# Sample search by sixteen candidates, two alternating row searches and whole queries in DRAM, in a two-layer hybrid decoder step

## The chip, the cores and the metric

The kernel runs on one core of one Trainium2 chip. The metric is device time in microseconds of one execution; the time of a kernel is the median of its runs. One further execution was taken by the hardware profiler, and all rows below are from that one.

## The reference

Layer 0 is a Mamba-2 branch beside a convolution branch. The change touches only layer 1, a sparse attention for 1024 prompt rows and, with the same weights, for 8 samples (one new row each, over 1024 cached keys and its own).

```
q, k, v, qi, ki, wi, z = odd_project(x, w_in)          # 1024-wide x times w_in
s = einsum('bthd,bsd->bths', qi, ki) * IDX_DIM ** -0.5   # 8 index heads of 64
scores = einsum('bths,bth->bts', relu(s), wi * IDX_HEADS ** -0.5)
scores = where(key_pos <= q_pos, scores, -inf)
_, idx = top_k(scores, 256)                             # per row
logits = einsum('btgrd,btkgd->btgrk', q, k_sel) * ATTN_HEAD_DIM ** -0.5
o = softmax(logits) @ v_sel                             # 16 heads, 4 groups of keys
y = layer_norm(ALPHA * x + (o * silu(z)) @ w_out)
```

## The kernel before

The program is written as Python loops; a scheduler puts the instructions of each engine into one fixed order before the run, and each engine then works through its own list in that order and waits where an operand is not there yet. A late operand therefore holds up everything behind it on the same engine.

Layer 1 (function `layer1`) starts near 905 us. Its first part, the front, ends near 1284 us and does three things side by side.

*Projections on TensorE (PE).* 66 pieces here called chunks, each 344 columns of one 128-row output tile: index queries QI (4 tiles of 3 chunks), queries QQ (8 tiles), keys KK (2 tiles), gates ZZ (8 tiles). fp32 accuracy is had by splitting weights and inputs in a high and a low half; a chunk is 24 matmuls (`mm3`, L132 to L134). The weights of a tile come in two parts; for each, a DMA fills `wst` (L105), ScalarE (ACT) casts the high half `whi` (L108), and VectorE (DVE), or GpSimd (POOL) where `eng=` says so, subtracts to get the low half `wlo` (L109). L132 and L133 need `whi`, L134 needs `wlo`. Queries are split in the same way as they leave PE: ACT casts the high half (L1113), DVE subtracts (L1114), and both halves go to `dq` in DRAM. Keys are split by L1132 (ACT) and L1133 (DVE), gates leave by L1186 (ACT).

*Scores.* For each block of 128 prompt rows (blocks 7 to 2; `SCORE_ROWS`), 8 index heads and up to two stretches of keys: two matmuls (L1033, L1034; 80 such pairs), relu on ACT (L1036), weighting and summing on DVE (L1040 and its neighbours) into `S`. The samples' scores come behind all blocks (matmuls L1068 to L1089) into `Ss`, 8 rows of 1025.

*Top-k by bisection on the bits of the 256th largest score.* Blocks 7, 6, 5 are searched on DVE (`topk_halves`, L1264 and what follows). Blocks 4, 3, 2 (search "a") and the samples (search "s") are searched on ACT and POOL by `topk_signs`: per bit, ACT takes the sign of score minus candidate and sums it over the row (L1231: three instructions `jka` of 640, 512 and 384 columns for "a", one `jks` of 1025 for "s"), and POOL turns the sums into the next candidate (L1236, L1250, L1251, L1253). 32 bits each. Then `masks` on DVE turns thresholds into 0/1 masks (L1306 counts, L1330 to L1334 scan and combine), in the order d, a, s.

The attention behind it goes through the blocks from 7 down. For each block and each of 4 key groups, `load_q` fetches the two halves of the queries from `dq` (L1139, into one of two `Q` buffers), PE makes logits (L1403), DVE applies the mask and takes the extremum (L1404), ACT the exponential (L1408), PE transposes and multiplies by V. POOL has the gates' products (L1465, L1467) and weight halves of the output projection (L1487). `sample_softmax` spreads the samples' masked scores over the heads by matmuls (L1578, L1584).

## Time and profile before

| | |
|---|---|
| median of 3 runs | 1689.2 us (1688.87 to 1689.37) |
| profiled execution | 1682.48 us, of which the span from first to last instruction is 1680.7 us |
| busy share of the span | PE 95%, DVE 70%, ACT 52%, POOL 20% |
| mean granted TensorE clock | 0.982 of full |
| DMA | 186.27 MB, mean 111 GB/s |
| layer 1 | front 905 to 1284 us, attention 1285 to 1681 us |

The busy shares are means over stages of different limits; what counts for the change is the front's second half, from the last score to the first logits.

### The profile page before, as it was taken

Reading aid. Unit: us, or ns where it says so; the run is one execution under the profiler, and the core shown is the slowest. Engines: PE = TensorE matmul, PEld = TensorE weight load, DVE = VectorE, ACT = ScalarE, POOL = GpSimd, SP = SyncE. Lnnn points to the kernel's source line nnn. Section 1 sums busy time; section 2 is a strip of 40 time slices with the busy share of each in tenths; the row PEclk is TensorE's granted clock in tenths of the full one; section 3 lists DMA queues with packets and bytes.
Section 4 is the critical chain, followed back from the end, with each engine's and each line's share of the span. In section 5 each row is a group of like instructions: output and inputs, shape, how many; then the busy total and the mean of one; then the engine's idle time right before and its main releaser. Section 6 shows DMA issues by size and latency. Waiting matters only on the chain. (4 is left out here: it accounts for less than half of the span.)

```text
span 1680.7 us, 28833 instructions
## 1 busy us (share of the span) xinstructions
PE 1589.8 (95%) x10334; PEld 1430.6 (85%) x10334; DVE 1170.7 (70%) x2460; ACT 869.4 (52%) x1958; POOL 335.0 (20%) x677
## 2 busy tenths in 40 slices
PE   8999989989999998999899999888898899999997
PEld 7999989989999997998899999777897576666675
DVE  4788977551466878766575568999967866565574
ACT  5255423562445555444534455577775755456563
POOL 4000000001212225123422200144361411112120
PEclk9999989999999999999999999999999999999999
DMA  7332242354112146433531214422346424543351
GB/s 236 109 118 62 69 114 92 127 175 170 40 38 63 61 141 210 129 116 101 167 106 51 92 47 135 130 95 89 120 147 186 129 48 111 136 110 89 85 131 59
DMA packets 167235, 186.27 MB, mean 111 GB/s; under 512 B 20500, under 2 KB 131436, under 8 KB 166836
## 3 DMA queue, kind: packets, MB, share of 16 engines
q1 hardware_dynamic: 164436, 178.41, 36.0%
q0 software_dynamic: 1216, 4.37, 0.8%
q8 instruction: 81, 1.33, 0.3%
q10 hardware_dynamic: 1440, 1.65, 0.3%
q14 instruction: 62, 0.51, 0.1%
HBM read 132.43 MB, written 54.05 MB: 111 GB/s over the span
## 5 line engine op out<-in xcount | busy, mean ns | idle before, releaser
L132 PE MATMUL pp<-act,whi 128*128 128x344 f32 x1016 | 328.9, 325 | 12.6 <-ACT act L233 8.2
L134 PE MATMUL pp<-act,wlo 128*128 128x344 f32 x1016 | 330.2, 327 | 10.6 <-DVE wlo L109 10.6
L133 PE MATMUL pp<-act,whi 128*128 128x344 f32 x1016 | 329.4, 324 | 0.8 <-POOL act L726 0.6
L132 PEld LDWEIGHTS pp<-act,whi 128*128 128x128 f32 x1016 | 193.2, 191 | 15.7 <-ACT act L233 8.2
L134 PEld LDWEIGHTS pp<-act,wlo 128*128 128x128 f32 x1016 | 193.6, 191 | 13.2 <-DVE wlo L109 11.5
L133 PEld LDWEIGHTS pp<-act,whi 128*128 128x128 f32 x1016 | 193.1, 190 | 3.4 <-POOL act L726 0.9
L108 ACT CAST whi<-wst 128x512 fp32r<-128x512 f32 x150 | 92.1, 617 | 151.9 <-PE pp L133 69.1
L334 DVE SCALAR_TENSOR_TENSOR uv<-uv,cst,uv 128x1024 f32<-128x1024 f32 x120 | 157.8, 1315 | 2.6
L132 PE MATMUL pp<-yh,whi 128*128 128x344 f32 x412 | 135.4, 329 | 8.4 <-DVE ev L1114 3.9
L109 DVE TENSOR_TENSOR wlo<-wst,whi 128x512 fp32r<-128x512 f32 x104 | 71.3, 691 | 98.8 <-ACT whi L108 98.7
L134 PE MATMUL pp<-yh,wlo 128*128 128x344 f32 x412 | 134.4, 326 | 3.6 <-DVE wlo L109 3.4
L1404 DVE CUSTOM_DVE_ANT_0 P<-lg,w 128x512 f32<-128x512 f32 (+3 forms) x144 | 82.8, 597 | 52.7 <-PE lg L1403 49.0
L1403 PE MATMUL lg<-w,Q 128*128 128x512 f32 (+3 forms) x384 | 104.9, 379 | 9.2 <-DVE nmx L1404 9.0
L109 POOL TENSOR_TENSOR wlo<-wst,whi 128x512 fp32r<-128x512 f32 x46 | 60.9, 1326 | 155.8 <-ACT whi L108 144.7
L132 PEld LDWEIGHTS pp<-yh,whi 128*128 128x128 f32 x412 | 79.1, 192 | 13.1 <-DVE ev L1114 5.3
L1408 ACT ACTIVATE P<-P,mx 128x1024 f32<-128x1024 f32 (+3 forms) x64 | 63.3, 989 | 49.6 <-DVE mx L1407 46.4
L1403 PEld LDWEIGHTS lg<-w,Q 128*128 128x128 f32 x384 | 64.7, 196 | 28.2 <-DVE nmx L1404 15.6
L1430 PEld LDWEIGHTS tr<-cst,P 128*128 128x128 f32 x576 | 65.7, 143 | 26.5 <-issue 20.1
L1430 PE MATMUL tr<-cst,P 128*128 128x128 f32 x576 | 86.1, 283 | 1.3 <-DVE yo L1463 1.3
L1439 PE MATMUL pv<-ph,V 128*64 128x256 f32 (+1 forms) x640 | 82.8, 375 | 2.9 <-ACT ph L1435 1.4
L134 PEld LDWEIGHTS pp<-yh,wlo 128*128 128x128 f32 x412 | 79.0, 192 | 5.2 <-DVE wlo L109 4.4
L1231 ACT ACTIVATE jka<-S,canda 128x640 bf16<-128x640 f32 (+2 forms) x96 | 68.7, 716 | 20.4 <-POOL canda L1253 15.8
(583 smaller groups left out, 3986.0 us busy)
## 6 DMA issues: line engine op xcount, KB each, us to landing
wst<-in_W SPq DMA_DIRECT2D x166, 256.0 KB, 2.8
Q<-dq SPq DMA_DIRECT2D x64, 256.0 KB, 4.2
dq<-ev SPq DMA_DIRECT2D x48, 172.0 KB, 1.8
q<-in_ck SPq DMA_DIRECT2D x64, 128.0 KB, 2.3
vp<-in_cv SPq DMA_DIRECT2D x64, 128.0 KB, 2.4
xst<-in_xT SPq DMA_DIRECT2D x8, 516.0 KB, 10.2
dzb<-ob SPq DMA_DIRECT2D x24, 172.0 KB, 1.9
uv<-dzb SPq DMA_DIRECT2D x8, 516.0 KB, 4.5
```

Source lines behind the costliest of these rows:

```text
L108: nc.scalar.copy(hi, st)
L109: (eng or nc.vector).tensor_tensor(lo, st, hi.bitcast(F32), op=ALU.subtract)
L132: nc.tensor.matmul(out, wh, ah, start=(start and kt == kts[0]), stop=False)
L133: nc.tensor.matmul(out, wh, al, start=False, stop=False)
L134: last = nc.tensor.matmul(out, wl, ah, start=False, stop=(stop and kt == kts[-1]))
L334: nc.vector.scalar_tensor_tensor(out, x, w[:, j : j + 1], y, op0=ALU.mult, op1=ALU.add)
L1231: nc.scalar.activation(jk, s, AF.Sign, bias=cand.bitcast(F32)[:, j : j + 1], scale=-1.0, accum_out=cnt[:, j : j + 1])
L1403: mm = nc.tensor.matmul(lg, Q[:, 4 * a + r, :], KT[g][:, s0 : s0 + m], start=(a == 0), stop=(a == 1))
L1404: nc.vector.tensor_tensor_reduce(out=P[:, s0 : s0 + m], in0=lg, in1=M[tb][:, s0 : s0 + m], scale=-0.125, scalar=BIG, op0=ALU.add, op1=ALU. ...
L1408: nc.scalar.activation(P, P, AF.Exp, bias=mx[:, r : r + 1], scale=-1.0, accum_out=rsum[:, r : r + 1])
L1430: nc.tensor.transpose(p[:, a, r * 128 : r * 128 + 128], Ps[r][:, (sb + a) * 128 : (sb + a) * 128 + 128], k.ident)
L1439: nc.tensor.matmul(pv[64 * u : 64 * u + 64, 256 * pr + c0 : 256 * pr + c1], V[:, sb + a, g * 64 : g * 64 + 64], ph[:, a, c0:c1], start=(sb ...
```

## The change

1. The samples' scores are now spread over 128 partitions (16 copies of each sample's row) and made right behind the first row block. Their search takes 4 bits a round: each of the 16 copies tests another candidate. A round is one Sign on ACT (128x1025), a comparison on POOL, a small matmul that counts the fitting candidates (`same`, L1165), an ACT copy, and three POOL instructions. 8 rounds in place of 32; round i is placed behind query tile i. Some 30 small instructions at the start of layer 1 make its constants.
2. The search of blocks 4, 3, 2 becomes two, "a" (block 4) and "b" (blocks 3 and 2), whose bits are issued in turn, held back until the last relu; a cast per bit goes.
3. Queries go to DRAM whole, in one fp32 copy (24 DMAs of 172 KB, not 48). `load_q` fetches half the bytes into `qst` and splits there: an ACT cast (L1220) and a POOL subtraction (L1221), 128x512 each, for all 32 loads.
4. The low weight halves of QQ, KK and ZZ (36), those of the keys (12) and the small copies L1151 go from DVE to POOL.
5. `sample_softmax` reads `Ss` directly, without its three fp32 matmuls (six instructions in the trace). A reduction of DVE (QX) moves behind the searches.

```
-    dq = k.t(dram, [4, 8, 64, T], F32, "dq")
+    dq = k.t(dram, [4, 4, 64, T], F32, "dq")
...
+    p = pm(k)[:, :128]
+    nc.tensor.matmul(p, c1("r128")[:8], c1("r128")[:8], start=True, stop=True)
+    nc.scalar.activation(same, p, AF.Copy, scale=t8[:, 3:4])
...
+        if tb == SCORE_ROWS[0]:
+            sample_scores()
...
+    def topk_samples():
...
+        for n in range(8):
+            cnt, fit, d = one("cnt"), one("fit"), one("dig")
+            nc.scalar.activation(jk[:, :1025], Ss[:, :1025], AF.Sign, bias=cand.bitcast(F32), scale=-1.0, accum_out=cnt)
+            eng.tensor_scalar(fit, cnt, float(1025 - 2 * TOPK), None, op0=ALU.is_le)
+            p = pm(k)[:, :1]
+            nc.tensor.matmul(p, same, fit, start=True, stop=True)
+            nc.scalar.copy(d, p)
...
+                eng.tensor_scalar(by, d, step[:, n : n + 1], None, op0=ALU.mult)
+                eng.tensor_tensor(new, base, by, op=ALU.add)
...
+                eng.tensor_tensor(cand, base, ups[:, n + 1 : n + 2], op=ALU.add)
+            yield base
...
     for i in range(8):
-        w = load_w(k, A["W"][QQ + i])
+        w = load_w(k, A["W"][QQ + i], eng=nc.gpsimd)
         for t0, n in CH:
-            p = pp(k)
+            p = pp(k) if i < 3 else either()
             mm3(k, p, w, x1, t0, n)
-            hi, lo = ev(F32R), ev(F32R)
-            nc.scalar.copy(hi, p)
-            nc.vector.tensor_tensor(lo, p, hi.bitcast(F32), op=ALU.subtract)
...
+            q = ev()
+            nc.scalar.copy(q, p)
...
+        ts = next(ss)
...
-        w = load_w(k, A["W"][KK + i])
+        w = load_w(k, A["W"][KK + i], eng=nc.gpsimd)
...
+            for j in range(2):
+                kt, here, there = KT[2 * i + j], slice(64 * j, 64 * j + 64), slice(64 - 64 * j, 128 - 64 * j)
+                nc.gpsimd.tensor_tensor(kt[there, sl], kf[here], kt[here, sl].bitcast(F32), op=ALU.subtract)
+
     def load_q(tb, g):
+
+        st = k.t(QB, [128, 512], F32, "qst", 1).rearrange("p (h t) -> p h t", h=4)
+        for j in range(2):
+            nc.sync.dma_start(st[64 * j : 64 * j + 64], dq[g][:, :, tb * 128 : tb * 128 + 128].rearrange("h d t -> d h t"))
         q = qb()[:, :1024].rearrange("p (h t) -> p h t", h=8)
-        for j in range(2):
-            nc.sync.dma_start(q[64 * j : 64 * j + 64].bitcast(F32),
-                              dq[g][:, :, tb * 128 : tb * 128 + 128].rearrange("h d t -> d h t"))
+        nc.scalar.copy(q[:, 0:4], st)
+        nc.gpsimd.tensor_tensor(q[:, 4:8], st, q[:, 0:4].bitcast(F32), op=ALU.subtract)
         return q
...
-        w = load_w(k, A["W"][ZZ + i])
+        w = load_w(k, A["W"][ZZ + i], eng=nc.gpsimd)
...
-    a, d = blocks(ACT_ROWS), blocks(DVE_ROWS)
-    ta = topk_signs("a", 128, a)
+    a, b, d = blocks(ACT_ROWS[:1]), blocks(ACT_ROWS[1:]), blocks(DVE_ROWS)
+    sa, sb = topk_signs("a", 128, a), topk_signs("b", 128, b)
+    for n in range(32):
+        with tc.issue_after(relu.ins) if n == 0 else ExitStack():
+            ta, tb = next(sa), next(sb)
...
-            nc.tensor.matmul(lg, R8, Ss[:, hf * 512 : hf * 512 + 512], start=True, stop=True)
             x = SL[:, hf * 512 : hf * 512 + 512]
-            nc.vector.tensor_tensor(x, x, lg, op=ALU.add)
+            nc.vector.tensor_tensor(x, x, Ss[:, hf * 512 : hf * 512 + 512], op=ALU.add)
```

**Order on ACT, at the second and first chunks of the gate tile ZZ0.** Before, the Signs of "a" (`jka`) and "s" (`jks`) alternate between the gate evictions (L1186):

```order
L1186 ACTIVATE ev_11710<-pp_11685 128x344
L1231 ACTIVATE jks_14046,cnts_14045<-Ss_9952,cands_14038 8x1025
L1231 ACTIVATE jka_13007,cnta_13004<-S_9951,canda_12995 128x512
L108 CAST whi_11923<-wst_11921 128x512
L1186 ACTIVATE ev_11738<-pt_11713 128x344
L1231 ACTIVATE jks_14056,cnts_14055<-Ss_9952,cands_14048 8x1025
L1231 ACTIVATE jka_13009,cnta_13004<-S_9951,canda_12995 128x384
```

In the changed kernel, at the same tile, gate evictions are L1256, and the Sign of block 4 (`canda`) alternates with the two of blocks 3 and 2 (`candb`):

```order
L1256 ACTIVATE ev_11772<-pp_11747 128x344
L1302 ACTIVATE jka_13328,cnta_13327<-S_10005,canda_13309 128x640
L1256 ACTIVATE ev_11800<-pt_11775 128x344
L1302 ACTIVATE jka_13337,cntb_13336<-S_10005,candb_13320 128x512
L108 CAST whi_11881<-wst_11879 128x512
L1302 ACTIVATE jka_13339,cntb_13336<-S_10005,candb_13320 128x384
L108 CAST whi_12013<-wst_12011 128x512
L1256 ACTIVATE ev_11828<-pp_11803 128x344
```

The samples' Signs have gone from here; the last Sign of "a" and "b" now stands beside ZZ3's second chunk, with 13 gate chunks of PE behind it, where before it stood beside ZZ6.

**Order on POOL, beside the last query tiles.** Before, POOL had only the steps of the two searches there:

```order
L1236 TENSOR_SCALAR bya_12965<-cnta_12956,fstepa_12757 128x1
L1236 TENSOR_SCALAR bys_13960<-cnts_13955,fsteps_13738 8x1
L1253 TENSOR_TENSOR cands_13958<-lows_13959,bys_13960 8x1
L1251 TENSOR_TENSOR lows_13969<-cands_13958,lows_13969 8x1
L1250 CAST lows_13979<-fsteps_13738 8x1
```

Now weight halves (`wlo`) and the samples' steps (`bys`, `bases`, `cands`) stand between the steps of "a" and "b":

```order
L109 TENSOR_TENSOR wlo_11268<-wst_11265,whi_11267 128x512
L1307 TENSOR_SCALAR byb_13070<-cntb_13063,fstepb_12896 128x1
L1174 TENSOR_SCALAR bys_11143<-digs_11136,steps_10678 128x1
L1175 TENSOR_TENSOR bases_11142<-bases_11031,bys_11143 128x1
L109 TENSOR_TENSOR wlo_11373<-wst_11370,whi_11372 128x512
L1324 TENSOR_TENSOR candb_13068<-lowb_13069,byb_13070 128x2
L1179 TENSOR_TENSOR cands_11146<-bases_11142,upss_10679 128x1
L1232 COPY q_11713<-qs_9165 64x2x4 x2
L1307 TENSOR_SCALAR bya_13080<-cnta_13075,fstepa_12847 128x1
```

A search step that stands behind a `wlo` waits for it, and a `wlo` waits for the steps ahead of it.

**Order on PE, at the last scores.** Before, projection matmuls (L132 to L134) stand between the last score pairs (L1033, L1034):

```order
L133 MATMUL pp_10974<-yb_8238,whi_10964 128x344
L1033 MATMUL pt_10435<-ki_9191,Q_9860 128x384
L1034 MATMUL pt_10435<-ki_9192,Q_9860 128x384
L134 MATMUL pp_10974<-yh_8237,wlo_10965 128x344
L132 MATMUL pp_10974<-yh_8239,whi_10964 128x344
```

Now the last eight pairs (L1118, L1119) follow each other, and the first of the counting matmuls (L1165) comes behind them:

```order
L1118 MATMUL pt_10562<-ki_9233,Q_9901 128x384
L1119 MATMUL pt_10562<-ki_9234,Q_9901 128x384
L1118 MATMUL pt_10568<-ki_9233,Q_9902 128x384
L1119 MATMUL pt_10568<-ki_9234,Q_9902 128x384
L1143 MATMUL pt_10574<-ev_10576 128x512
L1165 MATMUL pm_10686<-fits_10682,same_9228 128x1
```

Counted over the whole order, 24.1 chunks stood ahead of the last score pair and 41.9 behind it; now 22.5 stand ahead and 43.5 behind.

## Rows read from the trace of the kernel before

**Rows 1.** Busy time of each engine (with its instructions) in stretches of layer 1, then the granted PE clock, the share of DMA time and GB/s. The four columns behind the window's length and PE are PEld, DVE, ACT and POOL. The second stretch is from the last scores to the end of the projections, the third the hand-over to attention.

```profile
1000.00:1060.00 60.00, 60.00 (x356) 56.97 (x355) 55.02 (x112) 35.55 (x77) 1.05 (x3) 1.00 0.39 117
1060.00:1284.00 224.00, 199.57 (x1363) 186.55 (x1361) 190.67 (x428) 153.51 (x361) 89.25 (x326) 0.96 0.39 117
1284.00:1310.00 26.00, 19.01 (x116) 12.59 (x116) 25.29 (x57) 13.81 (x19) 1.05 (x1) 0.80 0.79 226
1310.00:1660.00 350.00, 344.36 (x2298) 244.34 (x2295) 221.07 (x687) 203.60 (x451) 67.15 (x82) 1.00 0.42 102
```

**Rows 2.** PE's timeline: start, duration, line, and in brackets the idle time ahead and what ended it. Last score pair, two matmuls of the last chunk, first and fifth logits.

```profile
1070.38 0.38 PE L1034 MATMUL pt<-ki,Q 128*128 128x384 f32 x1
...
1282.73 0.32 PE L133 MATMUL pp<-yl,whi 128*128 128x344 f32 x1
...
1283.84 0.32 PE L134 MATMUL pp<-yh,wlo 128*128 128x344 f32 x1
...
1285.10 1.20 PE L1403 MATMUL lg<-w,Q 128*128 128x512 f32 x4
1290.96 0.80 PE L1403 MATMUL lg<-w,Q 128*128 128x512 f32 x1 [4.66 <-DVE nmx L1404]
```

**Rows 3.** What PE waits for between 1060 and 1285 us: total us, times, longest.

```profile
PE pt L134 <- DVE wlo L109: 6.4, 4, 3.8
PE pp L132 <- DVE ev L1114: 3.9, 5, 1.3
PE pp L134 <- DVE wlo L109: 3.4, 2, 2.6
PE pt L132 <- DVE w L1133: 2.6, 1, 2.6
```

**Rows 4.** PE's groups between 1070.4 and 1284.5 us: the samples' part of the work (L1166 is the samples' logits, L1068 and L1086 their scores).

```profile
L1166 PE MATMUL pt<-q,q 128*32 128x128 f32 x240 | 9.6, 276 | 0.0
L1068 PE MATMUL pt<-w,q 128*64 128x128 f32 x64 | 8.1, 292 | 0.0
L1086 PE MATMUL pt<-q,W 64*8 64x512 f32 x4 | 1.9, 590 | 0.0
```

**Rows 5.** ACT's groups between 1060 and 1285 us: busy us, mean ns of one, idle time ahead and what ended it.

```profile
L1231 ACT ACTIVATE jka<-S,canda 128x512 bf16<-128x512 f32 (+2 forms) x95 | 67.9, 715 | 20.4 <-POOL canda L1253 15.8 <-DVE S L1040 2.0 <-POOL canda L1248 1.8
L1231 ACT ACTIVATE jks<-Ss,cands 8x1025 bf16<-8x1025 f32 x32 | 36.7, 1148 | 2.8 <-DVE Ss L1091 1.8 <-POOL cands L1253 0.9
```

**Rows 6.** ACT's timeline late in search "a": a Sign that waited for POOL, the read of its sum, an eviction, a Sign, a weight cast, a Sign; each next one starts while the end of the one before is still shown.

```profile
1258.94 0.83 ACT L1231 ACTIVATE jka<-S,canda 128x640 bf16<-128x640 f32 x1 [0.69 <-POOL canda L1253]
1259.67 0.18 ACT L1231 ACTIVATION_READ_ACCUMULATOR jka<-S,canda 128x1 f32 x1
1259.76 0.44 ACT L1186 ACTIVATE ev<-pt 128x344 f32<-128x344 f32 x1
1260.10 0.71 ACT L1231 ACTIVATE jka<-S,canda 128x512 bf16<-128x512 f32 x1
1260.71 0.19 ACT L1231 ACTIVATION_READ_ACCUMULATOR jka<-S,canda 128x1 f32 x1
1260.81 0.60 ACT L108 CAST whi<-wst 128x512 fp32r<-128x512 f32 x1
1261.32 0.61 ACT L1231 ACTIVATE jka<-S,canda 128x384 bf16<-128x384 f32 x1
```

**Rows 7.** POOL: the step L1236 of search "a" between 1060 and 1243 us (DVE busy nearly throughout) and between 1245 and 1285 us (DVE mostly idle), and the weight halves that POOL makes in layer 0.

```profile
L1236 POOL TENSOR_SCALAR bya<-cnta,fstepa 128x1 int32<-128x1 f32 x67 | 30.2, 452 | 27.4 <-ACT jka L1231 26.5
...
L1236 POOL TENSOR_SCALAR bya<-cnta,fstepa 128x1 int32<-128x1 f32 x24 | 6.9, 290 | 14.8 <-ACT jka L1231 14.8
...
L109 POOL TENSOR_TENSOR wlo<-wst,whi 128x512 fp32r<-128x512 f32 x46 | 60.9, 1326 | 155.8 <-ACT whi L108 144.7
```

**Rows 8.** DVE's groups between 1060 and 1285 us that leave it with the change.

```profile
L109 DVE TENSOR_TENSOR wlo<-wst,whi 128x512 fp32r<-128x512 f32 x27 | 18.5, 687 | 17.1 <-ACT whi L108 17.1
L1114 DVE TENSOR_TENSOR ev<-pp,ev 128x344 fp32r<-128x344 f32 x14 | 7.2, 511 | 0.0
```

**Rows 9.** DVE's timeline: the last score sum, the end of masks "d", the first and last instruction of masks "a", the first count of masks "s".

```profile
1079.03 0.62 DVE L1040 SCALAR_TENSOR_TENSOR S<-cum,wi,S 128x384 f32<-128x384 f32 x1
...
1242.41 0.96 DVE L1334 TENSOR_TENSOR w<-cum,eq 128x768 bf16<-128x768 f32 x1
...
1272.92 0.88 DVE L1306 TENSOR_SCALAR_CACHE_REDUCE eq<-S,canda 128x640 bf16<-128x640 f32 x1 [9.66 <-POOL canda L1253]
...
1289.74 0.56 DVE L1334 TENSOR_TENSOR M<-cum,eq 128x384 bf16<-128x384 f32 x1
...
1291.43 1.27 DVE L1306 TENSOR_SCALAR_CACHE_REDUCE eq<-Ss,cands 8x1025 bf16<-8x1025 f32 x1
```

**Rows 10.** Attention: the transfers of Q over the whole kernel (KB each, median us from issue to landing), what SP, which issues them, waited for between 1310 and 1660 us, and the two POOL groups there whose place the new step L1221 shares.

```profile
Q<-dq SPq DMA_DIRECT2D x64, 256.0 KB, 4.2
...
SPq L1139 <- PE lg L1403: 83.6, 16, 11.5
...
L1467 POOL TENSOR_TENSOR yl<-yo,yh 128x256 fp32r<-128x256 f32 x28 | 22.5, 804 | 24.3 <-ACT yh L1466 23.8 <-DVE ph L1433 0.5
...
L1487 POOL TENSOR_TENSOR wl<-z,wh 128x1024 fp32r<-128x1024 f32 x6 | 14.2, 2374 | 25.7 <-ACT wh L1486 23.4 <-DVE mx L1407 2.3
```

**Rows 11.** The samples' spreading matmuls L1584: duration min/median/max in ns, first and last start.

```profile
L1584 PE MATMUL po<-Ss,cst x4: 587/640/692, 1318.8 to 1324.3; 8*128 8x512 f32 x4
```

More of the change, by code (lines that the diff above doesn't have):

```diff
@@ L1021, in layer1 @@
     WD = [128 * (tb + 1) for tb in DVE_ROWS]
+    kg = [ra(F32)[:, :1024].rearrange("p (j r x) -> p j r x", j=2, r=4) for _ in range(4)]
+    for j in range(8):
+        nc.sync.dma_start(kg[j // 2][:, j % 2], k.dki[j].rearrange("r p x -> p r x"))
     UP = pack(BF16, ra, WD)
     S = k.t(sc_pool, [128, 4608], F32, "S")
-    Ss = k.t(ss_pool, [8, 1032], F32, "Ss")
+    Ss = k.t(ss_pool, [128, 1032], F32, "Ss")
     mask = c("mask")
+    QIP, W2 = S[:, :256], S[:, 256:384]
+    rS = k.t(QB, [128, 512], F32, "qst", 1)
@@ L1104, in either @@
         return pt(k)[:, :344] if turn[0] % 2 else pp(k)
+    def topk_samples():
+        eng = nc.gpsimd
+        one = lambda tag, dt=F32: k.t(tk, [128, 1], dt, tag + "s", 2)
+        sgn = k.t(tk, [128, 1], F32, "sgns", 1)
+        step, ups = k.t(tk, [128, 8], F32, "steps", 1), k.t(tk, [128, 8], I32, "upss", 1)
+        cand, base = first[:, 0:1], None
+        jk = ra(BF16, "ki")
+        for n in range(8):
[5 more added lines that the diff above has]
+            nc.scalar.copy(d, p)
+            new = one("base", I32)
+            if n == 0:
+                signed(new, d, (one("pos"), one("room"), one("minus", I32)), sgn)
+                eng.tensor_scalar(step, weight, sgn, None, op0=ALU.mult)
+                eng.tensor_scalar(ups, cands, sgn, None, op0=ALU.mult)
+            else:
+                by = one("by", I32)
+                eng.tensor_scalar(by, d, step[:, n : n + 1], None, op0=ALU.mult)
+                eng.tensor_tensor(new, base, by, op=ALU.add)
+            base = new
+            if n < 7:
+                cand = one("cand", I32)
+                eng.tensor_tensor(cand, base, ups[:, n + 1 : n + 2], op=ALU.add)
+            yield base
@@ L1221, in topk_signs @@
         fstep = k.t(tk, [R_, 31, n], F32, "fstep" + name)
+        istep = k.t(tk, [R_, 31, n], I32, "istep" + name)
         for bit in range(31):
@@ L1229, in topk_signs @@
             for j, (s, rows, w, _) in enumerate(bl):
[L1230 removed]
+                jk = k.t(sc_pool, [128, 640], BF16, "jka", 1)[:rows, :w]
                 nc.scalar.activation(jk, s, AF.Sign, bias=cand.bitcast(F32)[:, j : j + 1], scale=-1.0, accum_out=cnt[:, j : j + 1])
```

174 lines of the change are left out of this document (97 added, 77 removed).

## The prediction, made before the changed kernel ran

> **What bounds the kernel now.** I read the busy times by stretch first [rows 1]. From 1000 to 1060 us PE is busy throughout at the full clock. From 1060 to 1284 us, the end of the projections, it is busy 199.6 of 224 us, so idle 24.4, and its granted clock is 0.96, which on 199.6 us is another 8.0: some 32 us lost. In the hand-over, 1284 to 1310, it is busy 19.0 of 26 at 0.80: 7.0 idle and 3.8 of clock. Behind that, 1310 to 1660, it is busy 344.4 of 350 at full clock. So what can be won is lost between the last score and the first logits, and everything else is PE's own work.
>
> In the lossy stretch DVE is busy 190.7 of 224 us, ACT 153.5, POOL 89.3 [rows 1]. The waits of PE name DVE's products: low weight halves (6.4 and 3.4 us), the query split L1114 (3.9), the key split L1133 (2.6) [rows 3]. DVE is full there, because between these it searches blocks 7, 6, 5; its masks "d" end at 1243.4 [rows 9]. From then on ACT with POOL sets the end: DVE waits 9.66 us for search "a" until 1272.92, makes masks "a" until 1290.30, and only then takes the logits that PE had ready, so PE stands 4.66 us at 1290.96 [rows 2, 9]. Two limits follow one another: DVE first, the searches on ACT and POOL second.
>
> **The change part by part.** *PE, the floor.* The last score pair starts at 1070.38 [rows 2]. A projection matmul takes (1283.84 - 1282.73) / 7 = 0.159 us [rows 2]. Before, 41.9 chunks of 24 follow: 159.5 us, with the samples' logits 9.6 and scores 10.0 [rows 4], 179 us; with the 32 us lost this makes 211, and the trace has 213.7. In the changed order 43.5 chunks follow (165.6 us) and the logits (9.6), the samples' scores having moved ahead. If the last score stays at 1070.4, PE could end its projections at 1070.4 + 175.2 = 1245.6, against 1284.1.
>
> *When the last score comes.* The 1.6 chunks fewer ahead (6.1 us) stand against the samples' scores (10.0) ahead. DVE, which sums the scores until 1079.65 [rows 9], loses the splits in between and gets rounds of its own search in exchange. Bounds 8 us earlier and 6 later; I take no shift.
>
> *What is lost behind it.* Eight score pairs now follow one another without projection work. DVE needs 0.62 us a pair [rows 9], and a pass of its search may lie between; PE needs 0.36. Between 8 x 0.3 = 2 and 8 us; I take 4.
>
> A low half takes POOL 1.33 us, DVE 0.69 [rows 7, 8]. The 36 halves cost POOL 48 us, on top of 89.3 busy in 224 [rows 1]. Behind PE's use lie two parts of a tile in advance, so nothing is lost where POOL comes within a tile's 11.4 us; at worst each of 18 tiles waits for one half longer by 0.64 and for two search steps of 0.3, 22 us. Before, DVE cost PE 9.8 us by the same product [rows 3], with DVE at 85%. I take 3, nearer to nothing: 137 us of POOL in some 190 is 70%.
>
> ACT: the samples' 32 Signs were 36.7 us of it [rows 5]; 8 of 128 partitions and the same 1025 columns cost 9.2. Beside the searches of "a" and "b" the new order has 96 Signs, 20 weight casts, 46 small evictions, 7 sample Signs and one table load. A Sign of 640 columns costs 0.82 to the start of the next instruction, one of 512 0.71 [rows 6], the mean of the three is 0.72 [rows 5], and with the read of its sum (0.18) in full 0.90: 69 to 86, middle 76. A cast takes 0.51 and an eviction 0.34 to the start of the next [rows 6]: 10.2 and 15.6; the sample Signs 8.0, the load about 1. Sum 111 us. In the same stretch PE has 30.5 chunks and three of the eight sample groups, 116 + 4 = 120. So ACT has 9 us to spare for its waits on POOL, which before came to 17.6 us in one chain that paused 0.69 each bit [rows 5, 6]. Two alternating chains hide that pause (the other's Signs last 0.7 to 1.5 us), but the 20 weight halves of 1.33 us in POOL's queue do not fit under it: at up to 0.6 each 12 us. Bounds 0 and 14 us of loss on PE; I take 4.
>
> The eight counting matmuls hold PE if Sign and comparison are late: 0 to 1 us each, I take 1.5 in all. For the clock, which was 0.96 while PE had idle gaps and 1.00 where it had none [rows 1], I take 1.
>
> Sum 13.5: projections end at 1259, 25 us earlier.
>
> *Is DVE still behind PE?* Of the 27 low halves in 1060 to 1285 us about 22 lie ahead of 1243, with 14 query splits: 15.1 + 7.2 = 22 us off DVE [rows 8], and masks "d" end near 1221. Search "a" and "b" ends near 1080 + 120 = 1200 or, by the bounds, up to 1225. Masks of blocks 4 to 2 took 17.4 us for 1536 columns [rows 9], 11.3 ns a column, so the samples' 1025 take 11.6. 1221 + 17.4 + 11.6 = 1250, ahead of 1259. DVE is then free when the first logits come. The hand-over lost 10.8 us, 4.66 of it this wait, and masks "s" ran in it [rows 1, 2, 9]. I take 6 back (bounds 3 and 10).
>
> *Attention.* Six spreading matmuls go, four of 0.64 [rows 11]: 2.5 us of PE. Every load of Q gets an ACT cast of 0.5 and a POOL subtraction of 1.3. Q has two buffers, and SP waited 83.6 us for PE to release them [rows 10]; the transfer of 4.2 us then followed. Now the transfer goes ahead into `qst`, and behind the release stand cast and subtraction, 1.8 us and what is ahead of them in the queues, for example a weight half of 2.37 [rows 10]. So a load gets between 2.4 shorter and 2 longer. ACT had 204 and POOL 67 of 350 us [rows 1], so their 16 and 42 us fit. I take 3 lost (bounds -2 and 10).
>
> Sum: 25 + 6 + 2.5 - 3 = 30.5 us. The profiled execution took 1682.5 and the median is 6.7 above it; I carry the difference over: 1689.2 - 30.5 = 1658.7.
>
> **A rule weighed.** POOL's step took 0.45 us while DVE was nearly always busy and 0.29 when it was mostly idle [rows 7], so the two engines delay each other. The Trainium skill (SBUF — State Buffer, "SBUF: two separate sides") has a rule for this: GpSimd and VectorE hold a shared port pair for a whole instruction, and the other one blocks. The trace agrees in direction; no run here shows the port itself. By the row alone the 0.16 us on a step disappear under the other chain's Signs, and the sum stands; by the rule in full it would be that of the second rival.
>
> **Rivals.** *PE alone sets the end* (0.15). The losses of 13.5 shrink to 3 and the hand-over gives 9. For it speaks that all of [rows 3]'s names leave DVE. 30.5 + 10.5 + 3 = 44: 1645.
>
> *POOL sets the pace* (0.25). With DVE at 85% [rows 1], each of 20 low halves in the search stretch waits for half a DVE pass (0.9 to 1.3 us in [rows 9]), holds the chains, and the weights come late: 10 more on ACT's pace and 8 more on the halves. The rule above from the Trainium skill (SBUF — State Buffer) would make this the likely case. Against it: in layer 0 POOL made 46 such halves at 1.33 us and idled 144.7 us waiting for ACT's cast, so it was ready ahead of its input [rows 7]. 30.5 - 18 = 12.5: 1677.
>
> *The front gains and attention gives it back: slower* (0.08). ACT's cast stands in order ahead of exponentials and waits for PE's release of Q; if ACT then delays PE in each of 32 loads by cast, subtraction and the queue ahead, over 1.1 us more than I took, the gain is gone. At 1.8 it is 58 - 30.5 - 3 = 24 us longer: 1714. Against it: PE has hardly any wait there now, and the new wait is 1.8 where a transfer of 4.2 was.
>
> *The change doesn't do what it says* (0.05). The two chains don't cover each other: ACT waits for POOL 17.6 us as now [rows 5] and for the 20 halves in full, 26.6. ACT's stretch is then 111 + 44 = 155, PE's 120, and PE loses 35 where I took 4: 1689. Against it: neither chain needs the other's result, and in the new order POOL's steps of one stand ahead of the Signs of the other.
>
> **How the numbers follow.** The forecast has 0.47 with a range of its own from 1650 to 1670. The range reaches from PE alone (1645, less 2) to the pace of POOL and a little beyond (1683); below lie some 0.05, above 0.13. A measurement of this kernel can tell 0.2%, 3.4 us, from no change. Faster: 0.47 + 0.15 + 0.25 = 0.87; same 0.05; slower 0.08.
>
> **What would show it.** Right: projections end between 1250 and 1268, no wait of PE for DVE's low halves, the first L1404's successor within 2 us of its logits, DVE's masks "a", "b", "s" ended ahead of the first logits, PE idle under 14 us between scores and logits. Wrong: PE waiting over 8 us for POOL's `wlo`, ACT's Signs waiting over 30 us for POOL's candidates, or, in attention, logits waiting for Q's subtraction.

## The result, and the profile after

The changed kernel takes 1670.7 us (median of 4 runs, 1667.8 to 1674.9) against 1689.0 in the same comparison: a ratio of 0.9894, 95% interval 0.9872 to 0.9917. Run again later it gave 1668.6 and 0.9882 (0.9861 to 0.9902). The gain is 18 to 19 us; 30.5 were forecast. The first median lies 0.7 us above the range of the forecast itself (1650 to 1670), the second inside it. The profiled execution took 1667.78 us, with a span of 1666.0.

Busy times by stretch of the changed kernel, columns as in [rows 1]:

```profile
630.00:680.00 50.00, 42.17 (x257) 38.21 (x257) 38.66 (x102) 25.70 (x64) 23.13 (x13) 0.90 0.56 184
...
1000.00:1060.00 60.00, 60.00 (x378) 55.75 (x377) 38.36 (x71) 31.21 (x68) 7.96 (x6) 1.00 0.17 52
1060.00:1100.00 40.00, 33.42 (x162) 28.46 (x161) 39.31 (x90) 22.84 (x52) 15.89 (x50) 0.83 0.23 71
1100.00:1180.00 80.00, 79.95 (x535) 79.04 (x534) 76.92 (x156) 66.61 (x174) 65.92 (x180) 1.00 0.30 96
```

The same stretches of the kernel before (1000 to 1060 is in [rows 1]):

```profile
630.00:680.00 50.00, 43.10 (x284) 39.52 (x283) 41.29 (x116) 26.65 (x69) 22.20 (x12) 0.97 0.58 195
...
1060.00:1100.00 40.00, 35.35 (x217) 30.41 (x215) 38.71 (x105) 22.18 (x53) 8.99 (x42) 0.96 0.44 121
1100.00:1180.00 80.00, 66.53 (x396) 63.46 (x397) 77.44 (x177) 61.02 (x139) 33.46 (x145) 0.96 0.29 92
```

From 1100 to 1180 us PE has gone from 66.5 to 79.95 busy of 80, and POOL from 33 to 66. That is most of the gain. From 1060 to 1100 PE is worse than before: idle 6.6 us and a clock of 0.83. And layer 0, whose instructions are the same in both kernels, ran slower in this execution: its last matmul L856 starts at 893.0 against 887.5 before, with a clock of 0.90 against 0.97 in the stretch from 630 to 680. Counted from the start of that matmul, the projections end 378.2 us later, before it was 396.6, and the end of the span 773.0, before 793.2. So the layer gained 20.2 us, 5.5 of which the slower layer 0 hides in the spans.

What PE waits for between 1060 and 1285 us, the answer to [rows 3]:

```profile
PE pt L1118 <- ACT eq L1121: 3.4, 3, 1.4
PE pp L134 <- POOL wlo L109: 2.3, 1, 2.3
PE pm L1433 <- DVE ev L1431: 1.5, 2, 1.2
PE pt L1118 <- ACT cum L1121: 1.1, 1, 1.1
PE pm L1165 <- POOL fits L1163: 1.0, 1, 1.0
```

All waits of [rows 3] for DVE's splits are gone; POOL's low halves take 2.3 and 0.6 us where DVE's took 9.8. The largest wait is new: score pairs L1118 for the relu (L1121 on ACT), at the end of the scores. PE's timeline there:

```profile
1076.71 0.45 PE L1118 MATMUL pt<-ki,q 128*128 128x384 f32 x1 [1.35 <-ACT eq L1121]
...
1080.04 0.44 PE L1118 MATMUL pt<-ki,q 128*128 128x384 f32 x1 [0.98 <-ACT eq L1121]
...
1084.60 0.69 PE L1118 MATMUL pt<-ki,Q 128*128 128x384 f32 x1 [1.10 <-ACT eq L1121]
...
1086.56 0.79 PE L1143 MATMUL pt<-ev 1*128 1x512 f32 x1 [0.95 <-ACT cum L1121]
1088.31 0.58 PE L1165 MATMUL pm<-fits,same 128*128 128x1 f32 x2 [0.96 <-POOL fits L1163]
```

These are the last of the eight pairs without projection work between them. PE stops before most of them, and from 1080.4 us on its instructions are longer as well: the granted clock stood at its lower level, 1.2 GHz, for 13.7 us (a pair's matmul of 384 columns takes 0.69 us at 1084.60, 0.44 before).

DVE's masks, the answer to [rows 9]: the ends of masks "d", "a", "b" and "s", and the first mask step of the attention:

```profile
1240.16 0.96 DVE L1405 TENSOR_TENSOR w<-cum,eq 128x768 bf16<-128x768 f32 x1
...
1249.18 0.83 DVE L1405 TENSOR_TENSOR w<-cum,eq 128x640 bf16<-128x640 f32 x1
...
1260.94 0.56 DVE L1405 TENSOR_TENSOR M<-cum,eq 128x384 bf16<-128x384 f32 x1
...
1270.14 1.23 DVE L1405 TENSOR_TENSOR Ss<-cum,eq 128x1025 f32<-128x1025 f32 x1
...
1275.76 0.68 DVE L1488 CUSTOM_DVE_ANT_0 P<-lg,w 128x512 f32<-128x512 f32 x1
```

Nothing of DVE waits for a search any more (9.66 us before). But masks "d" end at 1241.1, hardly ahead of the 1243.4 of before, and all masks end at 1271.4, when PE ends its projections: the two engines are equally long, where the prediction had DVE 9 us ahead. Counted from the end of layer 0, masks "d" end at 348.1 us against 355.8, so 7.7 us earlier and not 22.

### The profile page after: what moved, and what is told of

It reads as the page before. It is cut to its first block, busy times and chain, and to the rows that moved or that the text cites. A ratio compares the mean times of both kernels' runs of the same rounds, so it can differ in the third digit from the quotient of the medians.

```text
span 1666.0 us, 28812 instructions
## 1 busy us (share of the span) xinstructions
PE 1587.4 (95%) x10346; PEld 1429.8 (86%) x10346; DVE 1163.0 (70%) x2380; ACT 861.4 (52%) x1951; POOL 425.2 (26%) x750
## 3 DMA queue, kind: packets, MB, share of 16 engines
q8 instruction: 81, 1.33, 0.3%
## 5 line engine op out<-in xcount | busy, mean ns | idle before, releaser
L132 PE MATMUL pp<-act,whi 128*128 128x344 f32 x1016 | 330.0, 327 | 13.3 <-ACT act L233 8.0
L134 PE MATMUL pp<-act,wlo 128*128 128x344 f32 x1016 | 330.9, 328 | 11.1 <-DVE wlo L109 11.1
L132 PEld LDWEIGHTS pp<-act,whi 128*128 128x128 f32 x1016 | 193.9, 191 | 16.8 <-ACT act L233 8.0
L134 PEld LDWEIGHTS pp<-act,wlo 128*128 128x128 f32 x1016 | 194.1, 191 | 13.7 <-DVE wlo L109 11.9
L109 POOL TENSOR_TENSOR wlo<-wst,whi 128x512 fp32r<-128x512 f32 x82 | 111.7, 1364 | 288.9 <-ACT whi L108 277.7
L134 PE MATMUL pp<-yh,wlo 128*128 128x344 f32 x348 | 111.6, 321 | 2.3 <-POOL wlo L109 2.3
L132 PE MATMUL pp<-yh,whi 128*128 128x344 f32 x348 | 112.0, 322 | 0.0
L109 DVE TENSOR_TENSOR wlo<-wst,whi 128x512 fp32r<-128x512 f32 x68 | 46.7, 696 | 83.2 <-ACT whi L108 82.9
L351 ACT ACTIVATE cft<-cw,own 128x80 f32<-128x80 f32 x256 | 66.2, 349 | 20.5 <-PE pt L353 12.2
L132 PE MATMUL pt<-act,whi 128*128 128x344 f32 x232 | 74.0, 321 | 0.0
L133 PE MATMUL pt<-act,whi 128*128 128x344 f32 x232 | 73.9, 320 | 0.0
```

The lines of the kernel that those rows point to most:

```text
L109: (eng or nc.vector).tensor_tensor(lo, st, hi.bitcast(F32), op=ALU.subtract)
L132: nc.tensor.matmul(out, wh, ah, start=(start and kt == kts[0]), stop=False)
L133: nc.tensor.matmul(out, wh, al, start=False, stop=False)
L134: last = nc.tensor.matmul(out, wl, ah, start=False, stop=(stop and kt == kts[-1]))
L351: nc.scalar.activation(wv[:, :, :, ch, :], taps2, AF.Copy, scale=own[:, ch : ch + 1])
```

## The experiments

Times of the kernel before lay between 1687.3 and 1688.1 in the four groups of runs. The changed kernel's own 1668.6 to 1670.7 is what the rest is compared with.

**1. Low halves back on DVE.**

```
-        w = load_w(k, A["W"][QQ + i], eng=nc.gpsimd)
+        w = load_w(k, A["W"][QQ + i])
...
-        w = load_w(k, A["W"][ZZ + i], eng=nc.gpsimd)
+        w = load_w(k, A["W"][ZZ + i])
```

> The changed kernel with one part undone: the 36 low weight halves of QQ, KK and ZZ are made by DVE again. Theory (DVE is the second bound of the front: in the trace of the changed kernel it is over 95% busy from 1060 to 1271 us and finishes its masks within 3 us of PE's last projection): DVE gets 36 x 0.69 = 25 us back, some 20 of them behind the last score, so its masks end 15 to 20 us later and the kernel takes 1683 to 1690 us. Rival (PE alone is the bound and DVE had room): within 4 us of the changed kernel's 1671. Rival (POOL's low halves hold up the searches and stretch DVE's instructions, so undoing helps): under 1667.

Measured: 1690.6, ratio 1.0024 (1.0010 to 1.0038). All of the gain is gone. Its waits of PE, 1080 to 1300 us:

```profile
PE pt L134 <- DVE wlo L109: 9.8, 5, 3.8
PE pp L134 <- DVE wlo L109: 7.6, 4, 3.7
```

The time came out just above the 1683 to 1690 of the theory, but its mechanism fell: masks "s" end as far behind layer 0 as in the changed kernel (378.5 us against 378.4), not 15 to 20 us later. All nine waits lie between 1105 and 1236 us. One of them, on ACT, DVE and PE:

```profile
1115.41 1.12 ACT L108 CAST whi<-wst 128x512 fp32r<-128x512 f32 x2
```

```profile
1116.52 1.28 DVE L1335 TENSOR_SCALAR_CACHE_REDUCE jkd<-w,candd 128x1024 bf16<-128x1024 bf16 x1
1117.84 1.15 DVE L1335 TENSOR_SCALAR_CACHE_REDUCE jkd<-w,candd 128x896 bf16<-128x896 bf16 x1
1119.03 1.01 DVE L1335 TENSOR_SCALAR_CACHE_REDUCE jkd<-w,candd 128x768 bf16<-128x768 bf16 x1
1120.20 0.69 DVE L109 TENSOR_TENSOR wlo<-wst,whi 128x512 fp32r<-128x512 f32 x1
1120.94 0.65 PE L134 MATMUL pt<-yh,wlo 128*128 128x344 f32 x1 [3.82 <-DVE wlo L109]
```

The casts are done at 1116.02 and 1116.54, and three search passes stand ahead of the low half. From 1080 to 1240 us a low half begins 4.8 us (median) behind the end of its cast here, 0.4 us where POOL makes it. That is not DVE's load, which is the same: busy times from 1080 to 1240 us in the kernel before, in the changed kernel and here, columns as in [rows 1] (DVE's time stands behind PEld's):

```profile
1080.00:1240.00 160.00, 138.74 (x905) 129.52 (x904) 154.43 (x341) 116.41 (x270) 72.82 (x268) 0.96 0.37 115
```

```profile
1080.00:1240.00 160.00, 153.24 (x1050) 146.59 (x1051) 154.00 (x298) 121.74 (x308) 114.23 (x319) 0.96 0.39 120
```

```profile
1080.00:1240.00 160.00, 137.58 (x848) 130.72 (x849) 154.15 (x326) 120.10 (x300) 94.30 (x301) 0.90 0.32 96
```

DVE is busy 154 of 160 us in all three, so it had no time to spare where PE waited (its longer pauses here come behind 1274.4, when its masks are done). How it can be as full without the low halves as with them: from the end of layer 0 to the end of masks "s" the changed kernel and this one have the same instructions on DVE, but for 35 low halves (24.0 us). The others took 16.6 us longer in sum where POOL made the halves; 22 of them were longer by over 0.3 us, and 17 of these, with 13.6 us, overlapped a low half on POOL. So moving the halves gave DVE back only 7.4 of 24.0 us. What PE gained is that the halves no longer stand behind search passes.

**2. One chain for blocks 4, 3, 2.**

```
-    a, b, d = blocks(ACT_ROWS[:1]), blocks(ACT_ROWS[1:]), blocks(DVE_ROWS)
-    sa, sb = topk_signs("a", 128, a), topk_signs("b", 128, b)
+    a, d = blocks(ACT_ROWS), blocks(DVE_ROWS)
+    sa = topk_signs("a", 128, a)
```

> The changed kernel with one part undone: blocks 4, 3, 2 are searched in one chain of 32 bits, not in two alternating ones. Theory (the search is hidden: it ended near 1220 us, 21 us ahead of DVE's masks d): a pause of some 0.7 us a bit comes back, 22 us, the search ends near 1240, still no later than masks d, and the time stays within 4 us of 1671. Rival (ACT's pace sets PE's evictions or the masks): 1678 or more, with ACT's Signs as what PE or DVE waits for.

Measured: 1671.6, ratio 0.9909 (0.9890 to 0.9927). The last Sign comes 25 us later behind layer 0, and the time is the same within the intervals, as the theory said. The alternation of the chains is worth nothing that can be told here.

**3. Queries in halves again.**

```
-            q = ev()
-            nc.scalar.copy(q, p)
+            hi, lo = ev(F32R), ev(F32R)
+            nc.scalar.copy(hi, p)
+            nc.vector.tensor_tensor(lo, p, hi.bitcast(F32), op=ALU.subtract)
```

(and `dq` and `load_q` as before the change)

> The changed kernel with one part undone: queries go to DRAM as two halves again, split by ACT and DVE, and are fetched as two halves. Theory (DVE is a bound of the front): 24 splits of 0.51 us return to DVE, some 7 us of them behind the last score, the rest where DVE was idle ahead of it; attention loses the ACT cast and the POOL subtraction of each load and gets back transfers of 256 KB. Sum 3 to 8 us longer, 1674 to 1679. Rival (the split in attention cost more than it brought): 1664 to 1669.

Measured: 1679.4, ratio 0.9946 (0.9927 to 0.9964). What ACT (first row) and PE wait for, 1080 to 1296 us:

```profile
ACT qs L1197 <- DVE ev L1192: 12.2, 5, 4.4
...
PE pm L1165 <- POOL fits L1163: 6.7, 4, 2.6
PE pp L134 <- POOL wlo L109: 4.1, 3, 3.7
PE pt L132 <- ACT whi L108: 3.4, 1, 3.4
PE pp L132 <- DVE ev L1192: 3.2, 2, 1.7
```

This is the same mechanism through two queues: the split L1192 stands behind search passes on DVE, ACT's copy behind it waits 12.2 us, and with it the Sign, the comparison and the counting matmul, and the weight casts. In the traces the front lost 18 us and the attention, counted from its first logits, took 386.6 us against 391.4. That is 13 us together, where the medians differ by 9 to 11; the profiled execution was the slowest of the seven. So the split in the attention costs some 5, and the whole queries pay by the front. The 4.8 is good to a few us only: the seven profiles with this attention and POOL's split took 389.7 to 394.1 in it, the two with queries split in the front 386.0 and 386.6. The time came out just above the theory's 1679, and the loss shows in the queues.

**4. Samples' scores behind the last row block.**

```
-        if tb == SCORE_ROWS[0]:
+        if tb == SCORE_ROWS[-1]:
             sample_scores()
```

> The changed kernel with one thing moved: the samples' scores stand behind the last row block, not behind the first. Theory (10 us of PE work ahead of the other scores starve DVE between 1000 and 1060 us, where it was 38 of 60 us busy against 55 before, and push its search and the last score out; PE then empties for 4.7 us at the end of the scores and its clock halves): the last score pair comes 8 to 12 us earlier, PE's idle and clock losses there (some 10 us) shrink to under 5, and the kernel takes 1662 to 1667. Rival (where the work stands does not matter since PE has to do it anyway): within 3 us of 1671.

Measured: 1669.1, ratio 0.9889 (0.9868 to 0.9911). The last pair did come 10 us earlier (182.1 us behind the end of layer 0, against 192.1), and the projections ended where they had (378.5 against 377.9 for their last matmul). The theory fell: when the last score comes doesn't matter, since PE has the samples' 10 us either ahead of it or behind. DVE did gain: its masks "s" ended 7.8 us earlier behind layer 0 (370.6 against 378.4), and then it waited 7.5 us for PE's last projection. The rival, "within 3 us", is what came.

**5. The kernel before with the low halves on POOL alone.** (`eng=nc.gpsimd` in the three `load_w` of QQ, KK, ZZ, on the kernel before.)

> The kernel before with one part done alone: the 36 low weight halves of QQ, KK and ZZ are made by POOL. Undoing this part cost 19 us and undoing the whole queries 8.7, 28 together where the change gained 18, so they are not independent. Theory (what counts is that no small product for PE or ACT waits in DVE's queue between search passes; the query splits L1114 and key splits L1133 are still there, and POOL now has 32 rounds of two searches besides): 1680 to 1688. Rival (the low halves alone are the gain): 1668 to 1675. Rival (POOL is too full with the samples' 32 rounds): 1690 or more, with PE waiting for POOL's low halves.

Measured: 1696.9, ratio 1.0060 (1.0042 to 1.0079): slower. The gain of the low halves is there only with the other parts. PE's waits, 1060 to 1305 us:

```profile
PE pp L132 <- ACT qs L1119: 7.8, 3, 3.5
PE pt L132 <- ACT whi L108: 6.0, 1, 6.0
PE pp L132 <- DVE w L1133: 3.8, 2, 3.1
PE pp L132 <- DVE ev L1114: 3.5, 4, 1.5
PE pt L132 <- DVE w L1133: 3.0, 1, 3.0
```

The low halves are no longer among the large ones (0.8 us), but the other splits are: ACT's copies L1119 stand behind the query splits on DVE, and PE's waits for them and for the key splits L1133 grew (7.8 against 1.6 and 6.8 against 4.3). The time is not that of the theory (up to 1688); the third case's time came, but PE does not wait for POOL's low halves, as that case had it. In the changed kernel those splits had left DVE too; that this is why the halves pay there is argued from the waits, and no run moves the other splits alone.

**6. The samples' search in 32 rounds.** The changed kernel with the samples' scoring, search, masks and spreading matmuls of the kernel before.

> The changed kernel with one part undone: the samples are scored behind the last row block on 8 partitions and searched in 32 rounds, with the matmuls in sample_softmax back. Theory (ACT and POOL had room for 36.7 and some 30 us in the first kernel's order, but now POOL also makes the low halves): POOL's queue gets 32 x 0.9 us more between low halves, the searches end 25 to 35 us later and masks s come behind PE's last projection; 2.5 us of PE return: 1676 to 1686. Rival (the samples' search was hidden and is hidden again): 1671 to 1674, just the matmuls.

Measured: 1681.5, ratio 0.9954 (0.9934 to 0.9975). DVE waits for it:

```profile
1280.90 1.27 DVE L1298 TENSOR_SCALAR_CACHE_REDUCE eq<-Ss,cands 8x1025 bf16<-8x1025 f32 x1 [26.72 <-POOL cands L1245]
```

Masks "s" start at 1280.9, at the end of the projections. Undoing it costs 11 to 13 us, as the theory said, though the search ends 58 us later behind layer 0 and not 25 to 35. The 32 rounds stand behind "a" and "b" here (Signs from 1205.5 to 1279.0), not beside them as in the kernel before (1096.4 to 1199.3). So this prices the short search against 32 rounds in this order, with the 2.5 us of matmuls; 32 rounds beside "a" and "b" were not tried.

**7. Queries split once, by POOL, in the front.**

```
+            hi, q = ev(F32R), ev(F32R)
+            nc.scalar.copy(hi, p)
+            nc.scalar.copy(q.bitcast(F32), p)
+            nc.gpsimd.tensor_tensor(q, q.bitcast(F32), hi.bitcast(F32), op=ALU.subtract)
```

> A version that might beat both: the changed kernel, but each query chunk is split once, in the front, with two ACT copies and one POOL subtraction, and both halves go to DRAM and are fetched as before. In the aligned traces the attention took 391.4 us from its first logits with the split in it and 386.6 without, and the front needs DVE free of the split. Theory: front as in the changed kernel, attention as with halves: 1664 to 1668. Rival (POOL, 82% busy from 1100 to 1180 us, can't take 24 x 0.9 us more, and ACT 24 evictions more): PE waits for POOL's low halves, 1674 or more.

Measured: 1670.4, ratio 0.9900 (0.9873 to 0.9927), the same as the changed kernel, so neither case's time. Its attention took 386.0 us from its first logits, as hoped, and its front gave that back: the first logits came 12.6 us later behind layer 0, with waits of PE for POOL's low halves of 5.2 us (2.9 in the changed kernel) and for the relu of 6.6 (4.5).

**8. Samples last, and DVE's search held until the last relu.**

```
+    with tc.issue_after(relu.ins):
+        td = topk_halves("d", d)
```

> The changed kernel with the samples' scores behind the last row block and DVE's search held back until the last relu has been issued. Theory (search passes of 1.1 us between the score sums make PE wait at the end of the scores and halve its clock there, together about 10 us): the last pair comes 15 us earlier than in the changed kernel, losses there under 4 us, 1662 to 1666. Rival (the search has to be done anyway and now ends later; masks d end near 345 us behind the end of layer 0 against 335, masks s behind PE's last projection): 1674 to 1682.

Measured: 1668.8, ratio 0.9894 (0.9869 to 0.9919). Neither case's time. The edit did not hold the search back: its first pass starts at 1014.7 us, in the fourth at 1015.3, and the last pair came at 182.1 again. So it says nothing on the passes between the sums.

**9. The changed kernel again.**

> The changed kernel itself once more, as the reference for the experiments and to see how far one execution differs from another. Theory (the 5.5 us that its profiled execution lost in layer 0, whose instructions are the same, to the granted clock are chance): a median of 1668 to 1673, and layer 0 ends between 887 and 896 us in the profile. Rival (the change slows layer 0 itself): layer 0 ends above 892 us again, as it did in seven of the eight experiments' profiles.

Measured: 1668.6, ratio 0.9882 (0.9861 to 0.9902). The time is the theory's; layer 0 ended at 896.7, past its 896, as the rival had it. (In the profiles of the eight experiments its last matmul came at 889.5 to 896.1, in six of them above 892, not in seven.) Against the rival speak the fifth experiment, all but the kernel before, with 894.9, and the seventh, tenth and twelfth, near the changed kernel, with 888.4 to 889.8. With one profile of each a small effect of the change on layer 0 is not ruled out.

**10. Query tile 3 in buffers of its own.**

```
-            p = pp(k) if i < 3 else either()
+            p = pp(k) if i < 4 else either()
```

> The changed kernel with query tile 3 kept in the buffers pp, as tiles 0 to 2 are, and not alternating with the buffers pt that the score pairs use. In the order 1.5 projection chunks then stand between the last eight score pairs again, as before the change. Theory (PE's stop of 6 us at the end of the scores, and the clock that halves there for 13.7 us, come from having nothing to do between those pairs): PE's losses there shrink from 10 to under 3 us, 1662 to 1667. Rival (the losses only move, since DVE and ACT then hand on the scores no faster): within 3 us of the changed kernel.

Measured: 1665.9, ratio 0.9868 (0.9844 to 0.9892), 3 to 5 us better than the changed kernel, within the overlap of the intervals. The stretch at the end of the scores, and PE's largest wait, between 1060 and 1285 us:

```profile
1060.00:1100.00 40.00, 38.07 (x220) 34.90 (x219) 39.14 (x89) 23.35 (x56) 19.12 (x51) 1.00 0.36 107
```

```profile
PE pm L1433 <- DVE ev L1431: 10.0, 1, 10.0
```

PE is 38.1 of 40 us busy there at full clock, not 33.4 at 0.83, and the last projection comes 9 us earlier behind layer 0 (368.7). Then PE waits 10.0 us for DVE, which has yet to end masks "s" and the reduction QX (L1431), and the first logits come when they did (381.2 against 381.6). Two bounds of equal length: in experiment 4 DVE gained and waited for PE, here PE gains and waits for DVE. What it waits for is QX, a small product, and DVE's queue has it behind masks "s":

```profile
1265.06 1.23 DVE L1405 TENSOR_TENSOR Ss<-cum,eq 128x1025 f32<-128x1025 f32 x1
1267.82 1.07 DVE L1431 TENSOR_REDUCE ev<-q 128x64 f32<-128x256 f32 x2
```

Without that wait PE could have begun its logits sooner, but DVE, busy without a pause over 0.5 us until 1270.85, could not have taken them. QX ahead of the masks alone was not tried.

**11. The split in `load_q` by DVE.**

```
-        nc.gpsimd.tensor_tensor(q[:, 4:8], st, q[:, 0:4].bitcast(F32), op=ALU.subtract)
+        nc.vector.tensor_tensor(q[:, 4:8], st, q[:, 0:4].bitcast(F32), op=ALU.subtract)
```

> The changed kernel with one instruction per load moved: the low half of a query block in load_q is subtracted by DVE, not by POOL. Theory (attention lost 4.8 us to the split, by the step on POOL of 1.3 us and its queue): DVE takes 0.69 us and is 62% busy there, attention from its first logits takes 387 to 390 us against 391.4, and the kernel 1666 to 1670. Rival (DVE's queue in attention is the closer one, it makes the mask step that PE waits for): 392 us or more, 1671 to 1676.

Measured: 1660.8, ratio 0.9841 (0.9819 to 0.9864), the lowest median of all, 8 to 10 us below the changed kernel where 1 to 5 were expected. The attention took 387.2 us from its first logits, near the 386.0 and 386.6 without any split in it. In the twelfth experiment, with the same split, it took 389.4. So it was in the main POOL's step that cost there, but by which path is not shown: no wait of PE in the attention of the changed kernel names Q's subtraction. The attention gives only some 4 us. In the profile, of this kernel's slowest run, the first logits come 2.8 us later behind layer 0 and the end 1.3 us earlier than in the changed kernel; where the rest of the 8 to 10 us comes from stays open.

**12. Four together.** Experiments 4, 10 and 11, and QX with its matmuls back ahead of the gate projections.

> The changed kernel with four things moved together: the samples' scores behind the last row block (as in the fourth experiment), query tile 3 in the buffers pp (tenth), the low half in load_q by DVE (eleventh), and the reduction QX with its two small matmuls back ahead of the gate projections. Theory (at the end of the front PE and DVE are two bounds of equal length, so that a gain for one alone is lost in waiting for the other: with scores late DVE's masks ended 8 us earlier and PE no earlier, with tile 3 in pp PE's projections ended 9 us earlier and the logits no earlier; both together must give it): projections end 367 to 372 us and the first logits 370 to 375 us behind the end of layer 0, attention takes 387 to 390 us, and the kernel 1650 to 1658, below the 1660.8 of the eleventh experiment. Rival (the gains don't add): 1659 to 1664.

Measured: 1687.4, ratio 1.0002 (0.9989 to 1.0015): everything lost. PE's waits, 1060 to 1310 us:

```profile
PE pm L1256 <- DVE ev L1254: 14.7, 1, 14.7
PE pp L132 <- ACT whi L108: 11.0, 2, 6.1
```

The projections ended at 401.1 us and the first logits came at 402.4 (forecast 367 to 372 and 370 to 375); the attention took 389.4, as forecast. One small matmul (L1256, 64x8), placed in PE's queue ahead of 24 gate chunks, waits 14.7 us for a reduction that stands behind search passes on DVE. In the kernel before, the same matmul at the same place waited half a microsecond; DVE's order there was another. Of the 11.0 us for weight casts, 5.0 are ACT's: a cast of a `load_q` (L1220) stands ahead of the weight cast in ACT's queue and waits 5.8 us for its transfer, and PE with it:

```profile
1103.79 0.62 ACT L1220 CAST Q<-qst 128x512 fp32r<-128x512 f32 x1 [5.76 <-DMA qst<-dq]
```

The other 6.1, at 1227.2 us, come behind Signs of the search, which here ended 19 us later behind layer 0 than in the changed kernel. Whether the other three gains add up stays open.

## Why the prediction came out as it did

**Right.** The direction, the place (between the last score and the first logits) and the price of most parts, though the main case's own range (1650 to 1670) was missed by a little in the first comparison. PE no longer waits for DVE's splits, the search ends ahead of masks "d" (last Sign near 1220; 1200 to 1225 was forecast), the samples' search has left the end. Of the signs named in advance, the first logits are taken within 2 us, all masks end ahead of them, and PE is idle 7 us between scores and logits (under 14); none of those for "wrong" came (2.9 us of waits for POOL's `wlo`, 13.8 for POOL's candidates, none for Q's subtraction). The projections' end, 1271.3, missed its window (1250 to 1268); without layer 0's 5.5 us it would lie in it. Of the losses, POOL's low halves cost 2.9 us (3 taken), the counting matmuls 1.0 (1.5 taken). Hand-over and spreading matmuls brought 9.0 (395.6 to 386.6 in the third experiment's attention; 8.5 forecast), and the split in the attention took 4.8 back (3 taken). These two are differences of single profiles, and such a difference can be off by a few us (experiments 3 and 9).

**Where the missing 10 to 12 us are.** From the end of layer 0 the projections gained 18.4 us, not 25; between their end and the first logits 2.4 were lost, since QX and its matmuls now stand there (the waits for L1431 above); the split in the attention took 1.8 more than forecast. In the front three terms of the sum were wrong. Counted from the end of layer 0, the forecast had the projections' end at 371.5 us, a floor of 358.1 and losses of 13.5; the profile has 361.8 and 16.7. That the losses come so near is in part luck: the end of the scores cost more than twice what was taken, and ACT's pace nearly nothing.

*The floor.* "I take no shift" for the last score pair was the first: it came 9.2 us later behind layer 0 than before, outside the bounds of -8 and +6. That the shift costs nothing by itself is what experiment 4 showed; the fault was to build the floor on it. PE's work is what stays. Taking idle time and halved clock out, from the end of layer 0 to that of the projections, leaves 363.4 us before and 361.8 now. The losses on top were 33.5 and are 16.7.

*The end of the scores.* I took 4 for it and 1 for the clock. It cost 6.6 us of idle time and some 5 of clock: of the stretches shown, 1060 to 1100 is the one where the changed kernel is worse. Experiment 10 shows the cause, the order in which no projection stands between the last pairs, and takes most of the loss away (1.9 us idle, clock 1.00).

*ACT's pace.* I took 4; outside the scores PE waited 0.6 us for ACT's weight casts and for no eviction. That ACT was no limit is also what experiment 2 says.

**DVE "ahead of 1259".** The step that put DVE's end at 1250 failed by 21 us, 5.5 of them layer 0's. It took 22 us of splits off DVE and left the rest of its work as long as it was. Two causes against it are in the rows: from 1000 to 1060 us DVE was busy for 38.4 us, 55.0 before, since PE did the samples' scores and not the rows'; and with the halves on POOL the other instructions of DVE take 16.6 us longer (experiment 1; single steps below). Experiment 4 sizes the first: without it masks "d" end 9.6 us earlier behind layer 0 and masks "s" 7.8. So DVE ends with PE, and experiment 10's gain in PE's time stopped at DVE.

**The rivals.** *PE alone* did not come: there is still a loss of 16.7. *POOL sets the pace* gave a time (1677) 6 to 8 us above the measured one, nearer than the forecast, 10 to 12 below, but not by its mechanism: PE waited 2.9 us for low halves. That POOL and DVE delay each other, which it was built on, did come; most of it fell on DVE's instructions (16.6 us), not on the halves' way to PE. "A rule weighed" saw only POOL's steps in this and not DVE's. *Slower by the attention* had the right place; its price was 4.8, not 58. *It doesn't do what it says* did not come: the alternating chains do cover each other (ACT waits 13.8 us for POOL's candidates, 17.6 before, and in one chain the search ends 25 us later), but nothing waits for what they win.

**The parts are not a sum.** Undone one at a time, the low halves cost 20 us, the samples' search 11, the whole queries 9, the chains nothing: 40 us, of a change that brought 18. The low halves done alone cost 9.5. Moving the low halves, the query splits and the key splits each takes one kind of small product out of a queue of long search passes; PE and ACT work in order, so the one that is left holds them up nearly as much as all of them did: PE's waits for DVE's low halves alone are 17.4 us in experiment 1, those of [rows 3] 16.3. The key splits and copies L1151 on POOL, and QX's place, were not undone by themselves.

## What to carry to other kernels

Where an engine in order waits for a small product, look at what stands ahead of that product in its maker's queue, not at the maker's busy share alone: DVE was busy 154 of 160 us in the changed kernel and in experiment 1, while PE waited 2.9 us for low halves in the one and 17.4 in the other. Work that is moved to another engine does not come off the first in full where the two lengthen each other's instructions: here 7.4 of 24.0 us. Build a floor from the whole work of the bounding engine between two fixed points, not from a moment in between that the change can shift. And when one engine's loss is mended, check that the next one isn't just as long before counting the gain.

## What the runs showed of the hardware

POOL and DVE lengthen each other's instructions where they overlap. In the changed kernel POOL makes four low halves between 1223 and 1236 us, and DVE makes masks "d":

```profile
1222.98 3.49 POOL L109 TENSOR_TENSOR wlo<-wst,whi 128x512 fp32r<-128x512 f32 x2
1232.37 1.74 POOL L109 TENSOR_TENSOR wlo<-wst,whi 128x512 fp32r<-128x512 f32 x1 [5.90 <-ACT whi L108]
1234.30 1.91 POOL L109 TENSOR_TENSOR wlo<-wst,whi 128x512 fp32r<-128x512 f32 x1 [0.19 <-PE pt L1247]
```

```profile
1223.07 2.25 DVE L1403 SCALAR_TENSOR_TENSOR eq<-cum,needd,eq 128x1024 f32<-128x1024 f32 x1
...
1233.00 2.06 DVE L1405 TENSOR_TENSOR w<-cum,eq 128x896 bf16<-128x896 f32 x1
```

The first of these DVE steps took 1.29 us both before the change and in experiment 1, where DVE makes the low halves itself (it is the longest of the three in the rows below, with the duration as min/median/max); here it takes 2.25, and a low half 1.74 to 1.91 where POOL's mean in layer 0 was 1.33 [rows 7]. The Trainium skill (SBUF — State Buffer, "SBUF: two separate sides") says that, where the DVE instruction reads two inputs from SBUF or runs in a 2-port mode, one of the two holds the shared port pair for a whole instruction and the other blocks. The durations agree with that in direction (0.96 us more on DVE's step, 0.4 to 0.6 on a half); no run shows the port itself. The search passes, which read one tensor and give out a sum, were not lengthened: their median is 1.15 us in the changed kernel and in experiment 1 alike. The 36 halves took 1.41 us in the mean, 0.08 more than those of layer 0; the second rival had half a pass, some 0.5, for each of 20. The step before the change, and in experiment 1:

```profile
L1332 DVE SCALAR_TENSOR_TENSOR eq<-cum,needd,eq x3: 1020/1146/1293, 1228.1 to 1240.7; 128x1024 f32<-128x1024 f32 x1, 128x896 f32<-128x896 f32 x1, 128x768 f32<-128x768 f32 x1
```

```profile
L1403 DVE SCALAR_TENSOR_TENSOR eq<-cum,needd,eq x3: 1020/1145/1287, 1228.7 to 1242.1; 128x1024 f32<-128x1024 f32 x1, 128x896 f32<-128x896 f32 x1, 128x768 f32<-128x768 f32 x1
```

Layer 0, with the same instructions, ended anywhere between 887.5 and 896.7 us in the fourteen profiles, in part by how often the granted clock fell in it: the five with 24 us at the lower level ended at 887.5 to 891.5, the nine with 34 to 41 us at 892.0 to 896.7. A difference of a few us between two single profiles is within that, and phases were therefore compared from the end of layer 0.
